# Hybrid decoder layer on one core: the MLP's first product as seven block products too, both products in one hand-ordered stream, weight sums formed by adding transfers

## The chip, the cores and the metric

One core of a Trainium2 chip runs the whole kernel. The metric is the device time of one execution in microseconds. The kernel before was run three times: median 786.67 us (785.09 to 787.71). Its profiled execution took 787.25 us, with a span of 785.5 us in the trace.

Engines: TensorE (PE; its weight loads are shown as PEld), VectorE (DVE), ScalarE (ACT), GpSimd (POOL), and SyncE (SP), which here only issues transfers. Sixteen transfer engines move data between the chip's memory and the on-chip SBUF.

## The reference, cut to what matters

The layer takes `x` (512 tokens x 1024), normalises it, multiplies by `w_in`, runs windowed attention and a convolution module side by side, merges both by gates, and adds `merged @ w_out` to `x`. Then comes the MLP, with a hidden width of 4096:

```python
x = x + merged @ w_out[l]
hmid = jnp.square(jax.nn.relu(rms_norm(x, norm_mlp_g[l]) @ w_ff1[l]))
x = x + hmid @ w_ff2[l]
```

All inputs are float32. The kernel works in float32r and splits each operand into a high part (a copy rounded by the cast) and a low part (the rest); a product is hi x hi + hi x lo + lo x hi, so three matmuls stand for one.

## The kernel before, in words

Up to the merge the kernel puts its steps on a list with `at(position, step)`; the list is sorted by position and every engine gets its instructions in that order. One unit of position is a quarter of a 24-matmul tile of TensorE. From `w_out` on, the code before is written stage after stage, and the framework's scheduler and its tile pools set the order on each engine.

*w_out.* 512 output columns at a time: four banks of PSUM collect 128 tokens each, 8 k-tiles x 3 matmuls with 512 moving columns. The second half goes token tile by token tile, each followed by `residual` (add to x, squares), `x2_norm` (the norm's factor in small steps on VectorE, then the scaling) and, for tiles 0 and 1, `x2_trans` (transposes on TensorE, then the high part on ScalarE and the low part on VectorE).

*MLP.* The hidden width is done in four parts of 1024 (`part`). Each part has a first-product stage and a second-product stage.

- First product (FF1): 8 tiles of 128 hidden channels, each the plain product over k = 8 tiles x 3 matmuls (`mm_T`, L187 to L192): weights are stationary, the 512 tokens move. The first three tiles (`EARLY`) are done in halves of 256 tokens, with the transposes of token tiles 2 and 3 between them. Weights arrive by `stationary_tiles` (L160), one 512 KB transfer per half of 256 columns, and are split by `split` (L153: cast on ScalarE, subtraction on VectorE). `ff1_evac` (L1125) takes relu, square, the parts and the sums `aS` of the activations that the next stage needs.
- Second product (FF2): a 2x2 block product of Winograd's form with seven multiplications instead of eight. Blocks: 256 tokens x 512 hidden x 512 outputs. `product` (L1175) issues one multiplication as 24 matmuls with 512 moving weight columns. Sums of weight blocks (`tq`, `b12`) are made on VectorE (`sub`, and L1214), then split by `pieces_of` (L1098). `add` (L1192) adds the banks to x, and in the last part stores the output.

Weights come in on SP's queue alone; GpSimd does nothing after w_out.

Of the kernel before, what the change touches and what calls it, by code (L numbers as in the profile page):

```python
# [52 lines left out]
def tile_hybrid_block(  # L53
# [941 lines left out]
    banks = ["ln", "ln", "ln", "mm", "mm", "mm"]  # L995

    def bank(name):

        banks.append(banks.pop(0))
        return pool_of["mm"].tile([P, S], F32, name=name, tag=banks[-1])  # L1000

    mTh, mTl = mT["h"], mT["l"]
    p2.close()
    gp.close()


    ff = ctx.enter_context(tc.tile_pool(name="ff", bufs=1, reuse_waits="tile"))

    def row4k(name, dtype=F32):
        return ff.tile([P, D], dtype, name=name, tag="row", bufs=5)  # L1010

    def quarter(name, dtype=F32):
        return ff.tile([P, 4, S], dtype, name=name, tag="quarter", bufs=4)

    gmlp = row4k("gmlp")
    nc.sync.dma_start(gmlp, bc(norm_mlp_g[0], P))
    x1 = []
    for t in range(NT):
        x1_t = keep.tile([P, D], F32, name=f"x1_{t}", tag="at", bufs=4)
        nc.sync.dma_start(x1_t, x[t * P:(t + 1) * P, :])  # L1020
        x1.append(x1_t)
    x2Th = ff.tile([P, KD, S], F32R, name="x2Th")
    x2Tl = ff.tile([P, KD, S], F32R, name="x2Tl")

    def mm_rows(accs, pieces, ah, al, kk):

        n = len(pieces)
        for i in range(n):
            for j in range(kk):
                for t in range(NT):  # L1030
                    k = i * kk + j
                    mm_M(accs[t], ah(k, t), al(k, t), pieces[i][0][:, j, :], pieces[i][1][:, j, :], k == 0,
                         k == n * kk - 1)

# [223 lines left out]
```

## Time and profile before

| | |
|---|---|
| three runs | 785.09 to 787.71 us, median 786.67 |
| profiled execution | 787.25 us, span 785.5 us |
| TensorE busy | 774.8 us, 99% of the span |
| VectorE, ScalarE, GpSimd busy | 561.5, 404.2, 254.3 us |
| moved by transfers | 79.56 MB, mean 101 GB/s |
| MLP: from its first to its last matmul | 451.86 to 781.43 us |

How to read it: a matmul's time in the trace runs from its start to its modelled end, and the next one starts before that end, so TensorE's busy time only says that work was always under way. The step from one start to the next tells its rate. "Idle before" is the time an engine stood still just before an instruction, with the work that ended last before it named behind the arrow.

### The profile page before, as it was taken

The numbers are of one execution on the slowest core, as the hardware profiler recorded it, in microseconds if no ns is written. First come the engines' busy times: TensorE is split into PE (matmuls) and PEld (weight loads), VectorE is DVE, ScalarE is ACT, GpSimd is POOL, SyncE is SP. The second block draws the span as 40 slices with busy tenths as digits, with TensorE's granted clock in tenths as the row PEclk, the third lists the DMA queues.
The fourth block names the chain that finished last, engine by engine and source line by source line (L and its number), as shares of the span: only waits on it lengthen the run. The fifth ranks groups of instructions, "written<-read, shape, count | busy, mean of one in ns | idle before, by whom it ended". The sixth has DMA issues, their size and how long they took to land.

```text
span 785.5 us, 10448 instructions
## 1 busy us (share of the span) xinstructions
PE 774.8 (99%) x3960; PEld 658.8 (84%) x3960; DVE 561.5 (71%) x949; ACT 404.2 (51%) x683; POOL 254.3 (32%) x189
## 2 busy tenths in 40 slices
PE   7999999999999999999999999999999999999998
PEld 7989989898888888888888898888888888888886
DVE  5466978898888878876431886886578766885683
ACT  5535557667666655356233356544554365435640
POOL 4443978958575565434364000000000000000000
PEclk8999999999999999999999999999999999999999
DMA  7351040314132131613335343143224223331102
GB/s 258 103 190 54 1 161 20 116 54 135 53 109 81 55 107 55 214 56 105 108 108 187 101 144 132 54 160 108 84 77 161 66 96 108 108 106 54 40 15 107
DMA packets 64807, 79.56 MB, mean 101 GB/s; under 512 B 2980, under 2 KB 52180, under 8 KB 64758
## 3 DMA queue, kind: packets, MB, share of 16 engines
q1 hardware_dynamic: 64758, 78.91, 29.9%
q8 instruction: 31, 0.51, 0.3%
q14 instruction: 18, 0.15, 0.1%
HBM read 76.78 MB, written 2.12 MB: 100 GB/s over the span
## 4 chain that ended last, share of the span: by engine, by line
PE 92%; DVE 3%; POOL 2%; ACT 1%; DMA 1%; issue 1%; SPq 0%; DVEq 0%; POOLq 0%; ACTq 0%
PE ps_f L191 7%; PE ps_f L192 7%; PE ps_f L190 7%; PE ps_x L1189 4%; PE ps_x L1186 4%; PE ps_x L1188 4%; PE ps_ta L484 2%; PE ps_ta L486 2%; PE ps_g L484 2%; PE ps_ta L485 2%; PE ps_wo L198 2%; PE ps_wo L196 2%; PE ps_wc L486 2%; PE ps_wc L484 2%; PE ps_y L1189 2%; PE ps_y L1186 2%
## 5 line engine op out<-in xcount | busy, mean ns | idle before, releaser
L782 DVE SCALAR_TENSOR_TENSOR cv<-h,wcol,cv 128x512 f32<-128x512 f32 x208 | 147.5, 746 | 0.5
L191 PE MATMUL ps_f<-x2Tl,wh_f 128*128 128x512 f32 (+1 forms) x280 | 104.1, 372 | 0.1
L190 PE MATMUL ps_f<-x2Th,wh_f 128*128 128x512 f32 (+1 forms) x280 | 103.6, 371 | 0.2 <-ACT x2Th L208 0.2
L192 PE MATMUL ps_f<-x2Th,wl_f 128*128 128x512 f32 (+1 forms) x280 | 103.8, 371 | 0.0
L157 DVE TENSOR_TENSOR wl_f<-raw_f,wh_f 128x1024 fp32r<-128x1024 f32 x32 | 39.1, 1223 | 59.8 <-ACT wh_f L156 58.8
L156 ACT CAST wh_f<-raw_f 128x1024 fp32r<-128x1024 f32 x32 | 33.6, 1054 | 55.4 <-PE ps_f L191 37.0
L191 PEld LDWEIGHTS ps_f<-x2Tl,wh_f 128*128 128x128 f32 x280 | 52.7, 188 | 9.3 <-DVE x2Tl L209 0.3
L190 PEld LDWEIGHTS ps_f<-x2Th,wh_f 128*128 128x128 f32 x280 | 52.6, 188 | 9.4 <-ACT x2Th L208 0.5
L192 PEld LDWEIGHTS ps_f<-x2Th,wl_f 128*128 128x128 f32 x280 | 52.7, 188 | 9.1
L1109 ACT CAST wh_b<-b 128x1024 fp32r<-128x1024 f32 x24 | 25.3, 1056 | 40.4 <-PE ps_y L1189 13.1
L1096 DVE TENSOR_TENSOR wl_b<-b,wh_b 128x1024 fp32r<-128x1024 f32 x24 | 29.3, 1223 | 22.1 <-ACT wh_b L1109 22.1
L1109 ACT CAST wh_t<-t 128x1024 fp32r<-128x1024 f32 x24 | 24.9, 1054 | 35.4 <-DVE t L1096 15.5
L691 ACT ACTIVATE s<-s,negm 128x257 f32<-128x257 f32 (+1 forms) x64 | 30.4, 478 | 16.5 <-DVE negm L683 16.5
L196 PE MATMUL ps_q<-wh_q,uTh 128*128 128x256 f32 x128 | 36.6, 286 | 0.0
L198 PE MATMUL ps_q<-wh_q,uTl 128*128 128x256 f32 x128 | 36.2, 283 | 0.0
L197 PE MATMUL ps_q<-wl_q,uTh 128*128 128x256 f32 x128 | 36.2, 283 | 0.0
L715 DVE TENSOR_TENSOR pTl<-ptp,pTh 128x512 fp32r<-128x512 f32 x28 | 19.3, 690 | 23.4 <-ACT pTh L711 23.4
L774 POOL TENSOR_TENSOR side<-side,tap 128x512 f32<-128x512 f32 x24 | 31.1, 1298 | 13.6 <-ACT tap L773 13.6
L1096 DVE TENSOR_TENSOR wl_t<-t,wh_t 128x1024 fp32r<-128x1024 f32 x24 | 29.0, 1220 | 5.9 <-ACT wh_t L1109 5.4
L700 POOL TENSOR_TENSOR s<-s,r 128x1024 f32<-128x1024 f32 (+1 forms) x16 | 26.9, 1682 | 14.7 <-DVE r L695 14.7
L683 DVE CUSTOM_DVE_ANT_0 s<-sp,bias,rb_sink 128x256 f32<-128x256 f32 (+1 forms) x64 | 26.2, 446 | 5.2 <-PE sp L676 4.9
L1096 DVE TENSOR_TENSOR aSl<-ss,aSh 128x1024 fp32r<-128x1024 f32 x16 | 19.6, 1225 | 13.2 <-ACT aSh L1122 13.2
(298 smaller groups left out, 2306.2 us busy)
## 6 DMA issues: line engine op xcount, KB each, us to landing
raw_f<-in_w_ff_dram SPq DMA_DIRECT2D x32, 512.0 KB, 4.2
b<-in_w_ff_dram SPq DMA_DIRECT2D x32, 512.0 KB, 3.8
x<-in_x_dram SPq DMA_DIRECT2D x8, 512.0 KB, 5.4
raw_g<-in_w_in_dram SPq DMA_DIRECT2D x8, 512.0 KB, 4.5
raw_a<-in_w_in_dram SPq DMA_DIRECT2D x8, 512.0 KB, 3.5
raw_q<-in_w_in_dram SPq DMA_DIRECT2D x8, 512.0 KB, 4.8
raw_ta<-in_w_in_dram SPq DMA_DIRECT2D x8, 512.0 KB, 4.4
raw_tc<-in_w_in_dram SPq DMA_DIRECT2D x8, 512.0 KB, 3.6
```

The lines of the kernel that those rows point to most:

```text
L157: lo_eng.tensor_tensor(out=wl, in0=raw_ap, in1=wh.bitcast(F32), op=ALU.subtract)
L190: pe.matmul(ps, wh[:, k, :], ah[:, k, cols], start=(k == 0), stop=False)
L191: pe.matmul(ps, wh[:, k, :], al[:, k, cols], start=False, stop=False)
L192: pe.matmul(ps, wl[:, k, :], ah[:, k, cols], start=False, stop=(k == nk - 1))
L196: pe.matmul(ps, ah, wh, start=first, stop=False)
L198: pe.matmul(ps, al, wh, start=False, stop=last)
L484: pe.matmul(ps, wh[:, k, :], ah(k), start=(k == 0), stop=False)
L782: ve.scalar_tensor_tensor(out=cps[ct], in0=src, scalar=w, in1=cps[ct], op0=ALU.mult, op1=ALU.add)
L1096: ve.tensor_tensor(out=out, in0=a, in1=b, op=ALU.subtract)
L1109: se.copy(wh, half)
L1186: pe.matmul(banks[t], ah, wh[:, j, :], start=(first and h + j == 0), stop=False, skip_group_check=True)
L1189: pe.matmul(banks[t], al, wh[:, j, :], start=False, stop=(last and h + j == 2), skip_group_check=True)
```

## The change

1. The first product of the MLP becomes a 2x2 block product with seven multiplications as well. A block is 512 k x 512 hidden x 256 tokens; weights stay stationary, so each matmul now moves 256 columns (before 512). The sums and differences of the activations (`xS`, from the transposed tokens `cx`) are made once; the results are collected in four blocks `ca`, on which relu, square, parts and sums are then taken.
2. Both products use one routine (`products`). The MLP is eight stages (`PHASES`): even ones first product, odd ones second. In each stage the seven products come in the order 1, 7, 6, 2, 5, 4, 3 (in the first stage 1, 2, 7, 6, 5, 4, 3).
3. Sums of weight blocks are no longer computed by VectorE. A block is fetched into one of three 1 MB buffers (`BUF`); when its two halves have been cut, a transfer from GpSimd's queue with `accum_op` adds another weight block onto the buffer, which gives the next product's weights. Products 5, 6, 4 and 7 get their weights that way; per stage there are 8 fetches and 8 adding transfers of 512 KB.
4. Everything from w_out on is put on the positions list. Pieces go through four slots (`n % 4`). The plain w_out chunks join the ring of weight chunks.
5. The norm before the MLP takes its factor from ScalarE's square root with one correction step (`rsqrt_root`), where before three steps on VectorE were made.

In the rows below, `aSh`, `aSl` are high and low part of the activations' sums, `xSh`, `xSl` those of the tokens, `piece` a cut weight half, `raw_b` and `raw_q` the three buffers, `c` a block of `ca`.

TensorE in the first part of the MLP, before: the end of one hidden tile and the start of the next (`wh_f`, `wl_f` weights, `x2Th`, `x2Tl` tokens).

```order
L190 MATMUL ps_f_6_4829<-x2Th,wh_f_3_0_4825 128x512
L191 MATMUL ps_f_6_4829<-x2Tl,wh_f_3_0_4825 128x512
L192 MATMUL ps_f_6_4829<-x2Th,wl_f_3_0_4826 128x512
L190 MATMUL ps_f_7_4863<-x2Th,wh_f_3_1_4859 128x512
L191 MATMUL ps_f_7_4863<-x2Tl,wh_f_3_1_4859 128x512
L192 MATMUL ps_f_7_4863<-x2Th,wl_f_3_1_4860 128x512
```

The same engine now, in a first-product stage: product 7, from its first bank to its second.

```order
L1133 MATMUL ps_y_4470<-xSh,pieceh 128x256
L1133 MATMUL ps_y_4470<-xSl,pieceh 128x256
L1133 MATMUL ps_y_4470<-xSh,piecel 128x256
L1133 MATMUL ps_y_4471<-xSh,pieceh 128x256
L1133 MATMUL ps_y_4471<-xSl,pieceh 128x256
L1133 MATMUL ps_y_4471<-xSh,piecel 128x256
```

The moving operand has half the columns, and one bank holds two hidden tiles of 256 tokens.

VectorE in the first second-product stage, before (`t` and `b` the buffers of weight sums, `wl_t`, `wl_b` low parts of weights, `ps_x`, `ps_y` the banks):

```order
L1196 TENSOR_TENSOR x_1_4106<-x_1_4106,ps_x_0_4909 128x512
L1096 TENSOR_TENSOR wl_t_01_5000<-t_4946,wh_t_01_4999 128x1024
L1096 TENSOR_TENSOR t_4946<-b_0_5018,t_4946 128x2048
L1196 TENSOR_TENSOR x_2_4108<-x_2_4108,ps_y_0_4910 128x512
L1196 TENSOR_TENSOR x_3_4110<-x_3_4110,ps_y_0_4911 128x512
L1096 TENSOR_TENSOR wl_t_00_5023<-t_4946,wh_t_00_5022 128x1024
L1096 TENSOR_TENSOR wl_t_01_5039<-t_4946,wh_t_01_5038 128x1024
```

VectorE now, at the passage from a first-product stage to a second-product stage:

```order
L1108 TENSOR_TENSOR piecel_4271<-raw_b,pieceh_4268 128x1024
L1155 TENSOR_TENSOR c_4155<-c_4155,ps_y_4470 128x512
L1155 TENSOR_TENSOR c_4155<-c_4155,ps_y_4471 128x512
L1108 TENSOR_TENSOR piecel_4272<-raw_b,pieceh_4269 128x1024
L1181 TENSOR_TENSOR c_4153<-c_4153,c_4155 128x1024
L1108 TENSOR_TENSOR piecel<-raw_q_4275,pieceh 128x1024
L1176 TENSOR_TENSOR aSl<-c_4153,aSh 128x4x256
L1186 SCALAR_TENSOR_TENSOR c_4153<-c_4153,c_4156 128x1024
L1108 TENSOR_TENSOR piecel_4270<-raw_q_4275,pieceh_4267 128x1024
```

The 2048-element weight sums are gone; between the cuts of the next stage's pieces stand the additions from PSUM and the sums and low parts of the activations.

The diff, cut to the MLP:

```diff
-    def sub(out, a, b):
-        ve.tensor_tensor(out=out, in0=a, in1=b, op=ALU.subtract)
...
-                mm_T(ps, wh, wl, x2Th, x2Tl)
-                ff1_evac(ps, m)
...
-        product(lambda t: a_of(aE, None, t), pieces_of(b11, f"b11_{part}"), X, True, True)
-        add(0, 0, X, False)
-        tq = quarter(f"t_{part}")
-        sub(tq, b22, b12)
-        product(S_(0), pieces_of(tq, f"t3_{part}"), Y, True, True)
-        add(1, 1, Y, False)
-        ve.tensor_tensor(out=tq, in0=tq, in1=b11, op=ALU.add)
...
+    ORDER = [(1, 2, 7, 6, 5, 4, 3)] + [(1, 7, 6, 2, 5, 4, 3)] * (PHASES - 1)
+    BUF = {1: 0, 5: 0, 7: 1, 6: 1, 4: 1, 2: 2, 3: 2}
...
+    def fetch(ph, buf, i, j, h):
+        ks = slice(2 * h, 2 * h + 2)
+        nc.sync.dma_start(tl["raw"][buf][:, ks, :], block(ph, i, j)[:, ks, :])
+
+    def fetch_add(ph, buf, i, j, h):
+        ks = slice(2 * h, 2 * h + 2)
+        ge.dma_start(tl["raw"][buf][:, ks, :], block(ph, i, j)[:, ks, :], accum_op=ALU.add)
...
+    def piece_hi(n, buf, h):
+        se.copy(tl["ph"][n % 4], tl["raw"][buf][:, 2 * h:2 * h + 2, :])
+
+    def piece_lo(n, buf, h):
+        ve.tensor_tensor(out=tl["pl"][n % 4], in0=tl["raw"][buf][:, 2 * h:2 * h + 2, :],
+                         in1=tl["ph"][n % 4].bitcast(F32), op=ALU.subtract)
...
+    def products(ph, prod, n, h, t):
+
+        (wh, wl), (ah, al) = (tl["ph"][n % 4], tl["pl"][n % 4]), operand(ph, prod)
+        acc = acc_of(ph, prod, t)
+        first = prod in (1, 7, 2) and h == 0
+        for c in range(2):
+            k = 2 * h + c
+            if ph % 2 == 0:
+                for q in range(2):
+                    o, w = acc[:, 256 * q:256 * q + 256], slice((2 * t + q) * P, (2 * t + q) * P + P)
+                    for i, (b, a) in enumerate(((wh, ah), (wh, al), (wl, ah))):
+                        pe.matmul(o, b[:, c, w], a[:, k, :], start=(first and c + q + i == 0),
+                                  stop=(k == 3 and i == 2), skip_group_check=True)
+            else:
+                w = slice(t * P, t * P + P)
+                for i, (a, b) in enumerate(((ah, wh), (ah, wl), (al, wh))):
+                    pe.matmul(acc, a[:, k, w], b[:, c, :], start=(first and c + i == 0),
+                              stop=(k == 3 and i == 2), skip_group_check=True)
...
+    for ph in range(PHASES):
+        m = M0 + 28 * ph
+        order = ORDER[ph]
+        ff1 = ph % 2 == 0
+        for j, prod in enumerate(order):
+            p = m + 4 * j
+            for h in range(2):
+                n = 2 * (7 * ph + j) + h
+                s = p - (3.4 if prod == 6 else 5.9) + 2 * h
...
+                at(s, piece_hi, n, BUF[prod], h)
+                at(s + 0.75, piece_lo, n, BUF[prod], h)
+                for t in range(2):
+                    at(p + 2 * h + t, products, ph, prod, n, h, t)
+                d = s + 0.9
+                more = ph + 1 < PHASES
+                if prod == 1:
+                    at(d, fetch_add, ph, 0, 0, 1, h)
+                elif prod == 7:
+                    at(d, fetch_add, ph, 1, 0, 0, h)
+                elif prod == 6:
+                    at(d, fetch_add, ph, 1, 1, 0, h)
+                elif prod == 2:
+                    at(d, fetch, ph, 2, 1, 1, h)
+                elif prod == 5 and more:
+                    at(d, fetch, ph + 1, 0, 0, 0, h)
+                elif prod == 4 and more:
+                    at(d, fetch, ph + 1, 1, 0, 1, h)
+                    at(d + 4.5, fetch_add, ph + 1, 1, 1, 1, h)
+                elif prod == 3 and more:
+                    at(d, fetch, ph + 1, 2, 1, 0, h)
...
-    nc = _bacc.Bacc("TRN2", target_bir_lowering=False, num_devices=1, dynamic_dma_scratch_size=1024)
+    nc = _bacc.Bacc("TRN2", target_bir_lowering=False, num_devices=1, dynamic_dma_scratch_size=2048)
```

In the loop above a product is four units long, `p` is its position, a piece is cut 5.9 units ahead (product 6: 3.4), and the transfer that refills the buffer is issued 0.9 units after that.

## Rows read from the trace of the kernel before

**Rows 1.** The page: span; busy us of each engine with its share of the span and its count of instructions; the chain that ended last, by engine.
```profile
span 785.5 us, 10448 instructions
...
PE 774.8 (99%) x3960; PEld 658.8 (84%) x3960; DVE 561.5 (71%) x949; ACT 404.2 (51%) x683; POOL 254.3 (32%) x189
...
PE 92%; DVE 3%; POOL 2%; ACT 1%; DMA 1%; issue 1%; SPq 0%; DVEq 0%; POOLq 0%; ACTq 0%
```

**Rows 2.** All that TensorE waited for from 400 us to the end: engine, tile and line, then the releaser, then us in total, times, longest.
```profile
PE ps_f L190 <- ACT x2Th L208: 0.2, 1, 0.2
```

**Rows 3.** Busy us (and instructions) of PE, PEld, DVE, ACT and POOL in stretches of the span; then TensorE's granted clock as a share of 2.4 GHz, the busy share of the transfer engines and what they moved in GB/s. The first rows are four of the eight stretches from 452 to 782 us (the others read alike) and the sum over all eight; the stretch from 498.55 is the first of the four second-product stages.
```profile
452.00:500.00 48.00, 47.89 (x287) 42.76 (x288) 36.12 (x56) 27.94 (x42) 0.00 (x0) 1.00 0.34 115
...
540.00:580.00 40.00, 40.00 (x178) 33.12 (x177) 22.48 (x31) 21.61 (x31) 0.00 (x0) 1.00 0.25 79
580.00:620.00 40.00, 40.00 (x178) 33.15 (x177) 34.49 (x36) 18.37 (x19) 0.00 (x0) 1.00 0.38 132
...
740.00:782.00 42.00, 41.59 (x184) 34.12 (x182) 28.85 (x34) 13.55 (x16) 0.00 (x0) 1.00 0.19 69
sum 330.00, PE 329.49 PEld 275.67 DVE 236.60 ACT 159.50 POOL 0.00; mean PE 41.19 PEld 34.46 DVE 29.58 ACT 19.94 POOL 0.00
...
498.55:536.64 38.09, 38.09 (x170) 31.55 (x169) 32.73 (x34) 17.29 (x18) 0.00 (x0) 1.00 0.39 135
```

**Rows 4.** Instructions of TensorE in order of time: start, us of one, engine, line, operation, tiles, shapes. First and last of 38 wide matmuls in a row of w_out; then first and last of 22 narrow ones in a row of the MLP's first product.
```profile
435.62 0.39 PE L197 MATMUL ps_wo<-wout1l,mTh 128*128 128x512 f32 x1
...
444.01 0.39 PE L198 MATMUL ps_wo<-wout1h,mTl 128*128 128x512 f32 x1
...
452.81 0.28 PE L192 MATMUL ps_f<-x2Th,wl_f 128*128 128x256 f32 x1
...
455.32 0.28 PE L192 MATMUL ps_f<-x2Th,wl_f 128*128 128x256 f32 x1
```

**Rows 5.** Groups of TensorE by line and shape over the whole span, count (x) | busy us, mean ns of one | idle before: the first product's matmuls, two of the three lines that are wide and two of the three that are narrow, and a weight load.
```profile
L190 PE MATMUL ps_f<-x2Th,wh_f 128*128 128x512 f32 x232 | 90.3, 389 | 0.0
L192 PE MATMUL ps_f<-x2Th,wl_f 128*128 128x512 f32 x232 | 90.2, 389 | 0.0
...
L191 PE MATMUL ps_f<-x2Tl,wh_f 128*128 128x256 f32 x48 | 13.8, 288 | 0.1
L190 PE MATMUL ps_f<-x2Th,wh_f 128*128 128x256 f32 x48 | 13.3, 285 | 0.2 <-ACT x2Th L208 0.2
...
L190 PEld LDWEIGHTS ps_f<-x2Th,wh_f 128*128 128x128 f32 x280 | 52.6, 188 | 9.4 <-ACT x2Th L208 0.5
```

**Rows 6.** TensorE in order of time around the first matmuls of the MLP (ps_f) and at the third group of transposes (tp_m, x8 together), columns as in rows 4.
```profile
450.59 1.03 PE L206 MATMUL tp_m<-ident,u 128*128 128x128 f32 x8
451.86 0.62 PE L190 MATMUL ps_f<-x2Th,wh_f 128*128 128x256 f32 x3 [0.24 <-ACT x2Th L208]
452.59 0.38 PE L191 MATMUL ps_f<-x2Tl,wh_f 128*128 128x256 f32 x1
...
455.44 1.04 PE L206 MATMUL tp_m<-ident,u 128*128 128x128 f32 x8
456.24 0.36 PE L191 MATMUL ps_f<-x2Tl,wh_f 128*128 128x256 f32 x1
```

**Rows 7.** The end of the span in order of time: the last matmul and the last addition.
```profile
781.20 0.39 PE L1189 MATMUL ps_x<-wh_b,aSl 128*128 128x512 f32 x1
781.63 0.69 DVE L1196 TENSOR_TENSOR x<-x,ps_x 128x512 f32<-128x512 f32 x1 [2.03 <-PE ps_x L1189]
```

**Rows 8.** Groups of VectorE by line and shape from 380 us on, columns as in rows 5.
```profile
L1096 DVE TENSOR_TENSOR wl_b<-b,wh_b 128x1024 fp32r<-128x1024 f32 x24 | 29.3, 1223 | 22.1 <-ACT wh_b L1109 22.1
...
L1196 DVE TENSOR_TENSOR x<-x,ps_x 128x512 f32<-128x512 f32 x32 | 21.2, 682 | 7.6 <-PE ps_x L1189 7.6
L1096 DVE TENSOR_TENSOR aSl<-ss,aSh 128x1024 fp32r<-128x1024 f32 x16 | 19.6, 1225 | 13.2 <-ACT aSh L1122 13.2
...
L1096 DVE TENSOR_TENSOR t<-b,t 128x2048 f32<-128x2048 f32 x4 | 9.2, 2292 | 0.1
...
L1069 DVE SCALAR_TENSOR_TENSOR u<-x,y_m,gmlp 128x1024 f32<-128x1024 f32 x4 | 5.1, 1285 | 0.1
...
L114 DVE TENSOR_TENSOR a_m<-y_m 128x1 f32<-128x1 f32 x12 | 1.9, 159 | 0.4
```

**Rows 9.** The same for ScalarE.
```profile
L156 ACT CAST wh_f<-raw_f 128x1024 fp32r<-128x1024 f32 x32 | 33.6, 1054 | 55.4 <-PE ps_f L191 37.0 <-PE ps_x L1189 10.0 <-PE ps_z L1189 5.0
...
L1131 ACT ACTIVATE r<-ps_f 128x512 f32<-128x512 f32 x32 | 19.2, 599 | 1.0
...
L1041 ACT ACTIVATE fsq<-x 128x512 f32<-128x512 f32 x8 | 5.0, 629 | 7.0 <-DVE x L1039 7.0
L208 ACT CAST x2Th<-tp_m 128x512 fp32r<-128x512 f32 x8 | 4.5, 585 | 12.4 <-PE tp_m L206 12.4
...
L1041 ACT ACTIVATION_READ_ACCUMULATOR fsq<-x 128x1 f32 x8 | 1.5, 186 | 0.0
```

**Rows 10.** Transfers by tile: count, KB each, median us from issue to landing.
```profile
raw_f<-in_w_ff_dram SPq DMA_DIRECT2D x32, 512.0 KB, 4.2
b<-in_w_ff_dram SPq DMA_DIRECT2D x32, 512.0 KB, 3.8
...
out_dram<-x SPq DMA_DIRECT2D x8, 256.0 KB, 2.0
```

More of the change, by code (lines that the diff above doesn't have):

```diff
@@ new lines, in tile_hybrid_block, with load_x1, bank, wout_mm @@
+    x1 = []
+    def load_x1():
+        for t in range(NT):
+            x1_t = keep.tile([P, D], F32, name=f"x1_{t}", tag="at", bufs=4)
+            nc.sync.dma_start(x1_t, x[t * P:(t + 1) * P, :])
+            x1.append(x1_t)
+    at(WO + 3, load_x1)
+    at(W0 + 0.9, open_tail)
+    banks = ["ln", "ln", "ln", "mm", "mm", "mm"]
+    def bank(name):
+        banks.append(banks.pop(0))
+        return pool_of["mm"].tile([P, S], F32, name=name, tag=banks[-1])
+    def wout_mm(acc, k, t, wh, wl):
+        cols = slice(t * P, (t + 1) * P)
+        mm_M(acc, mT["h"][:, k, cols], mT["l"][:, k, cols], wh, wl, k == 0, k == KD - 1)
@@ new lines, in x2_trans, with x2_keep @@
+    def x2_trans(t, half):
+        tp = aux.tile([P, 4, P], F32, name=f"tp_m{t}{half}", tag="aux")
+        for j in range(4):
+            k = 4 * half + j
+            pe.transpose(tp[:, j, :], us[t][:, k * P:(k + 1) * P], ident)
+        tl["tp", t, half] = tp
+    def x2_keep(t, half):
+        se.copy(tl["cx"][2 * (t // 2) + half][:, :, (t % 2) * P:(t % 2) * P + P], tl["tp", t, half])
+    for i, u in enumerate(wout_uses):
+        for j in range(2):
+            at(W0 + 4 * i + 2 * j, wout_first, u, i, j)
@@ new lines, in row_add, with c_half @@
+    def row_add(ph, half_t, half_n, prod, t, minus, store):
+        n, cols = 2 * half_t + t, slice(half_n * S, half_n * S + S)
+        ve.tensor_tensor(out=x1[n][:, cols], in0=x1[n][:, cols], in1=acc_of(ph, prod, t),
+                         op=ALU.subtract if minus else ALU.add)
+        if store and ph == PHASES - 1:
+            nc.sync.dma_start(out[n * P:(n + 1) * P, cols], x1[n][:, cols])
+    def c_half(i, t):
+        return tl["ca"][i].rearrange("p (t q) c -> p t (q c)", t=2)[:, t, :]
@@ new lines, in operands, with open_x @@
+    def operands(x, p):
+        for key, pos in p.items():
+            if key[0] == "S":
+                at(pos, op_sum, x, int(key[1]))
+            else:
+                at(pos, op_hi, x, int(key[1]))
+                at(pos + 0.75, op_lo, x, int(key[1]))
+    def open_x():
+        cx = keep.tile([P, 2, 4, 256], F32, name="cx2", tag="act", bufs=2)
+        tl["cx"] += [cx[:, i] for i in range(2)]
+        tl["xS"] = [tl["pool"].tile([P, 4, 4, 256], F32R, name=f"xS{n}", tag="xS" + n) for n in "hl"]
@@ new lines, in open_a, with open_banks @@
+    def open_a(what):
+        if what == "S":
+            tl["aS"] = [keep.tile([P, 4, 4, 256], F32R, name=f"aS{n}", tag="act", bufs=2) for n in "hl"]
+        else:
+            w = 256 if what == "E" else S
+            tl["a" + what] = [tl["pool"].tile([P, 4, w], F32R, name=f"a{what}{n}", tag=f"a{what}{n}") for n in "hl"]
+    def open_banks():
+        x, y, z = ([bank(f"ps_{role}{t}") for t in range(2)] for role in "xyz")
+        tl["banks"] = ({"x": x, "y": y, "z": z}, {"x": z, "y": y, "z": x})
@@ L994, in tile_hybrid_block @@
             fn(*args)
[L995 to L1033, printed above, removed]
```

323 lines of the change are left out of this document (171 added, 152 removed).

## The prediction

> **What bounds the kernel now.** I read the page's busy shares and chain first. TensorE is busy for 774.8 of 785.5 us, and the chain that ended last lies 92% on it [rows 1]. Next the list of what TensorE waited for, from 400 us on, where w_out and the MLP lie: one entry of 0.2 us [rows 2]. So in the part that the change rewrites there is no wait to remove; only fewer or cheaper matmuls help, and every new wait on TensorE costs its full length. The granted clock is 1.00, the 2.4 GHz level, from 452 us on [rows 3].
>
> Busy time is no measure of a matmul here, since its rows overlap (390 ns long, started every 227 ns). I take the step between starts. A matmul with 512 moving columns: from 435.62 to 444.01 us lie 37 steps, 8.39 / 37 = 0.2268 us. One with 256 columns: from 452.81 to 455.32 lie 21 steps, 2.51 / 21 = 0.1195 us, so two narrow ones cost 0.239 us, 5% more than a wide one [rows 4].
>
> The profiled execution took 787.25 us, 1.75 more than its span and 0.58 above the median of 786.67. I make the sum against 787.25 and take the 0.58 off at the end.
>
> **The change part by part.** *First product of the MLP.* Before: 696 wide and 144 narrow matmuls (x232 and x48 on each of three lines, [rows 5]): 696 x 0.2268 + 144 x 0.1195 = 157.9 + 17.2 = 175.1 us. After: 4 stages of 7 products of 2 halves x 2 banks x 2 k-tiles x 2 column blocks x 3 = 48 narrow matmuls, 1344 in all: 1344 x 0.1195 = 160.6 us. The columns fall by an eighth (12.5%), the time by 8.3%, because all of them are now narrow. **Gain 14.5 us.** The narrow step is read from the same operation on the same operands, so I take it with little doubt.
>
> *Second product.* 4 x 7 x 24 = 672 wide matmuls before and after: 152.4 us, unchanged. Transposes: 32 before and after.
>
> *Check of the sum.* From the first FF1 matmul at 451.86 [rows 6] to the step after the last matmul at 781.20 [rows 7] are 329.6 us; 175.1 + 152.4 + two groups of eight transposes at 0.8 (455.44 to 456.24, [rows 6]) are 329.1. Nothing else is in this stretch.
>
> *w_out and the norm,* now in the written order with the rest. 192 wide matmuls as before, none of them with a wait [rows 2], so nothing to gain. The one place where before lost time is the eight transposes at 450.59 and what follows: the second FF1 matmul starts only at 452.59 where 0.8 + 0.12 us would do, about 1 us lost [rows 6]. After, the first product needs only the first 256 tokens, which come from token tiles 0 and 1; for these I count from the end of tile 1's w_out matmuls: add 0.68, square 0.82, some eight small steps of 0.16, scaling 1.29, transposes, copy 0.59, hi 1.05, lo 1.22: about 8 us, while two more token tiles give TensorE 2 x 24 x 0.2268 = 10.9 us [rows 8, 9]. Tile 3's own chain of about 4.9 us to its transposes lies beside product 1 (5.7 us). So the start is covered with one to three microseconds to spare; I put the 1 us gained against small new waits here and book zero.
>
> *VectorE* [rows 8]. Per pair of stages before: 59 us by these lines (236.6 us busy in the 330 us of [rows 3], of which a pair is a quarter). After: 28 weight cuts x 1.22 = 34.2, 7 low parts and 4 sums of activations x 1.23 = 13.5, 6 + 14 additions from PSUM x 0.68 = 13.6: 61.3 us of a pair's 78.3. The four weight sums of 2.29 each leave VectorE, 14 more cuts come. In the second-product stage alone: 14 cuts 17.1, 14 additions 9.5, 8 operand steps 9.8 = 36.4 us in a stage of 38.1, against 32.7 before in 38.1 (498.55 to 536.64, [rows 3]). That is tight (96%), but a cut is placed to end about one product (5.4 us) ahead of its use and the following first-product stage asks only for about 25 of 40 us. Cost zero; if the cover fails, see the rivals. *ScalarE:* 28 casts x 1.05, 7 operand casts and 7 relu or square at 1.05, 8 PSUM reads of 0.6 = 49 of 78.3 us [rows 9]: hidden.
>
> *Transfers.* This is the new part. Before, a pair of stages loads 8 MB once; after, each stage fetches eight 512 KB halves and adds eight more, so 16 fetches and 16 adds per pair. A plain 512 KB transfer: in 580 to 620 us the engines moved 132 GB/s at a share of 0.38, so 347 GB/s when busy, 1.51 us of all 16 [rows 3]; it lands 3.8 us after issue [rows 10]. No adding transfer is in the trace. Bound from below: the same as a fetch, 1.51 and 3.8 us. From above: three passes one after the other (read the weights, read the tile, write it back), 4.5 and 11.4 us. I take two, since the nearest rows are a fetch and, for reading the tile, the output's store, 2.0 us for 256 KB [rows 10]: 3.0 us of the engines, and 3.8 + 2 x 2.0 = 7.8 us to landing.
> Throughput for a pair at two passes: 16 x 1.51 + 16 x 3.02 = 72.5 us against TensorE's 160.6 / 4 + 152.4 / 4 = 78.3. Hidden, with 7% to spare.
> The tightest link: product 7 and product 6 follow one another and use the same buffer. Product 7's piece can be cut once TensorE has left the slot, 1.5 products (8.2 us) before its use; less cast, cut and handoffs (1.05 + 1.22 + 0.2) its buffer is free for the add 5.7 us before product 7. Product 6 begins 5.4 us after that and needs its own 2.5 us of cutting: 5.7 + 5.4 - 2.5 = 8.6 us for the add, against 7.8. All other adds have one and a half times that or more. The adds are issued from GpSimd, which does nothing else then. Behind a late piece the cast waits on ScalarE and the cut on VectorE, and behind these the next product's pieces, so a late add shows in full on TensorE.
> The Trainium skill, "Collectives: The Full Stack", section on the bandwidth ceiling, has a rule against this: an add made in the transfer takes two source reads, and its reduce ran at 1/1.93 of a copy. An estimate by that figure: a pair would ask 24.2 x 2.93 = 70.9 us of 78.3, so the transfers would still be hidden, but with no room for a second transfer to be late. No run here shows it yet.
>
> *Tail.* Last matmul, one addition (0.69 at 781.63, [rows 7]), one 256 KB store: the same.
>
> *Sum:* 787.25 - 14.5 = 772.75; less 0.58 for the median 772.2; I add 0.8 for waits at eight stage changes of 0.1 each. **773.0 us.**
>
> **The rivals.**
> *A: the adds become the bound (slower).* Place: the 16 transfer engines in all eight stages. With r passes per add a pair asks 24.2 x (1 + r). It exceeds 78.3 from r = 2.24; the gain of 3.6 per pair is gone from r = 2.39. At 2.5: 84.7, 6.4 x 4 = 26 us, 773 + 26 = 799 us; at three: 96.8, 74 us, 847 us. For it: the traffic doubles in a stretch whose share is 0.19 to 0.38 so far, a quarter of the adds is on an 8.6 us link, and nothing in the trace shows their rate. Against it: at one or two passes everything fits.
> *B: VectorE's second-product stage falls behind.* If each of its 36 instructions waits 0.15 us more on handoffs, the stage needs 41.8 us; up to 3.7 us x 4 = 15 us. With half of it covered by the lead: 781 us. For it: 96% and an in-order queue in which additions from PSUM stand before cuts. Against it: before ran 32.7 of 38.1 without one wait on TensorE.
> *C: the narrow stream does not keep 0.1195 us.* At 0.1303 the gain is zero, 787 us. For it: the weight is exchanged at every narrow matmul, 188 ns of load beside a 120 ns step [rows 5]. Against it: 144 of just these ran at that step.
>
> **How the numbers follow.** Forecast 0.68 (its own range 769 to 777), B 0.18, A 0.12, C 0.02. Within 0.3% means 784.3 to 789.0, about what can be told from no change. Faster: 0.68 and 0.13 of B, 0.81. Same: 0.03 of B and C, 0.05. Slower: A and 0.02 of B, 0.14. The range from 769 to 792 leaves out A and a little below.
>
> **What would show it.** Right: narrow matmuls 0.1195 us apart throughout the first-product stages, 40.1 us per such stage and 38.1 per other; TensorE's waits under 3 us from w_out on; transfer share 0.6 to 0.95 in the MLP. A would show as ScalarE's casts waiting for the adding queue and TensorE waiting for casts, most at product 6. B would show as TensorE waiting for cuts late in second-product stages, with VectorE above 95% there. The forecast falls if a stage takes over 42 us, or if the adds land later than 8.6 us.

## The result and the profile after

The changed kernel takes 790.2 us, median of 19 runs (786.71 to 794.59), beside 786.68 us for the kernel before (19 runs): ratio 1.0042, 95% interval [1.0029, 1.0056]. It is slower by 3.5 us, where 773.0 us was forecast. Its profiled execution took 788.5 us.

The page of the changed kernel: span, busy time, two transfer queues (packets, MB, share of 16 engines' span), the chain that ended last, and transfers with KB and median us from issue to landing.

```profile
span 786.7 us, 11648 instructions
...
PE 766.4 (97%) x4464; PEld 668.5 (85%) x4464; DVE 566.0 (72%) x888; ACT 438.6 (56%) x696; POOL 332.1 (42%) x253
...
q1 hardware_dynamic: 56566, 78.91, 30.7%
q0 software_dynamic: 17408, 33.56, 24.2%
...
PE 59%; DMA 13%; issue 10%; DVE 8%; POOL 6%; ACT 3%; POOLq 0%; SPq 0%; ACTq 0%; DVEq 0%
...
raw_q<-in_w_ff_dram SPq DMA_DIRECT2D x48, 512.0 KB, 6.3
raw_q<-in_w_ff_dram POOLq DMA_DIRECT2D x48, 512.0 KB, 7.7
```

Against [rows 1]: TensorE's busy time fell by 8.4 us and its idle time rose by 9.6. The chain was 92% TensorE; now it is 59%, and transfers, VectorE and GpSimd are on it. GpSimd's queue (q0) carries the adds: 33.56 MB took 24.2% of 786.7 us, 190 us of all engines, 176 GB/s.

What TensorE waited for from 380 us on (us in total, times, longest):

```profile
PE ps_z L1138 <- DVE piecel L1108: 5.4, 6, 1.0
PE ps_x L1133 <- ACT c L1152: 2.2, 1, 2.2
PE ps_z L1138 <- ACT pieceh L1105: 1.7, 1, 1.7
PE ps_x L1133 <- DVE piecel L1108: 1.3, 3, 0.8
PE ps_x L1133 <- ACT pieceh L1105: 0.3, 1, 0.3
```

Before there was 0.2 us here [rows 2]; now 10.9 us. Nearly all but the 2.2 us stands at the two halves of product 6, which begin some 11 and 14 us after a stage's start (the 2.2 us stands before product 5 of the first stage). Who holds up the pieces, from the list of waits of the other engines in the MLP (same columns):

```profile
POOL raw_q L1094 <- DMA raw_q<-in_w_ff_dram: 139.9, 20, 13.3
...
DVE piecel L1108 <- ACT pieceh L1105: 69.7, 39, 6.6
ACT pieceh L1105 <- DMA raw_q<-in_w_ff_dram: 51.5, 20, 4.3
```

ScalarE's casts wait 51.5 us for blocks that are not there yet, VectorE's cuts wait for these casts, and TensorE for the cuts. Counted through in the program's order, all 20 of these waits are for products 7, 6 and 4, which share the second raw buffer.

The MLP's eight stages (columns as in [rows 3]: length, busy us of PE, PEld, DVE, ACT, POOL, clock, transfer share, GB/s), first and second product in turn:

```profile
453.65:496.80 43.15, 40.98 (x347) 40.78 (x346) 32.48 (x37) 28.44 (x36) 8.46 (x7) 1.00 0.63 134
496.80:539.62 42.82, 39.39 (x170) 31.42 (x169) 35.40 (x37) 24.21 (x26) 10.49 (x9) 1.00 0.90 203
539.62:581.02 41.40, 40.30 (x337) 39.88 (x336) 23.62 (x24) 24.43 (x28) 10.12 (x9) 1.00 0.92 211
581.02:621.01 39.99, 39.04 (x170) 31.42 (x169) 35.17 (x37) 22.00 (x24) 9.68 (x8) 1.00 0.91 205
621.01:661.34 40.33, 40.08 (x337) 39.87 (x336) 22.96 (x24) 24.52 (x27) 9.69 (x8) 1.00 0.92 211
661.34:702.29 40.95, 39.20 (x170) 31.42 (x169) 34.84 (x37) 22.04 (x23) 9.68 (x8) 1.00 0.90 204
702.29:742.65 40.36, 40.01 (x338) 39.60 (x336) 23.02 (x25) 24.51 (x28) 9.69 (x8) 1.00 0.93 213
742.65:782.70 40.05, 39.06 (x170) 31.23 (x168) 32.27 (x34) 18.87 (x20) 4.84 (x4) 1.00 0.64 146
sum 329.05, PE 318.06 PEld 285.62 DVE 239.76 ACT 189.01 POOL 72.66; mean PE 39.76 PEld 35.70 DVE 29.97 ACT 23.63 POOL 9.08
```

Forecast were 40.15 and 38.1 us, 313 in all; it is 329.05, as long as the 329.6 us before. The last second-product stage asks less of the transfers than the others (share 0.64) and still takes 40.05.

**The loop of one buffer.** The second raw buffer serves product 7, then (by an add) 6, then (by an add) 4; after that a fetch and another add make it product 7's block of the next stage. One turn of its second half, as ScalarE's casts of it show (in order of time; start, us, idle before and releaser):

```profile
623.02 1.05 ACT L1105 CAST pieceh<-raw_q 128x1024 fp32r<-128x1024 f32 x1 [3.02 <-DMA raw_q<-in_w_ff_dram]
...
633.57 1.05 ACT L1105 CAST pieceh<-raw_q 128x1024 fp32r<-128x1024 f32 x1 [0.91 <-DMA raw_q<-in_w_ff_dram]
...
644.64 1.05 ACT L1105 CAST pieceh<-raw_q 128x1024 fp32r<-128x1024 f32 x1 [2.06 <-DMA raw_q<-in_w_ff_dram]
...
663.63 1.05 ACT L1105 CAST pieceh<-raw_q 128x1024 fp32r<-128x1024 f32 x1
```

Product 7's cast waits 3.02 us for the add, product 6's 0.91, product 4's 2.06. The adds between them as GpSimd issues them (same columns; the last row is both halves of the next product 7's add), and the landing of the last two (least, median, most):

```profile
625.75 1.20 POOL L1094 DMA_DIRECT2D raw_q<-in_w_ff_dram  x1 [1.31 <-DVE piecel L1108]
...
636.29 1.21 POOL L1094 DMA_DIRECT2D raw_q<-in_w_ff_dram  x1 [1.69 <-DVE piecel L1108]
650.74 2.44 POOL L1094 DMA_DIRECT2D raw_q<-in_w_ff_dram  x2 [13.24 <-DMA raw_q<-in_w_ff_dram]
...
DMA to landing us min/median/max: 8.0/9.8/11.6
```

The second half's add, issued at 652.0, lands 11.6 us later at 663.6, and the next product 7's cast starts at 663.63. ScalarE shows no idle time there, since its other work ends at the same moment. The turn is 10.55 + 11.07 + 18.99 = 40.61 us, one link right behind the other, and the stage that it spans 40.33. Nothing in it may be late, since the next turn starts from its end.

From this came three theories. **Loop:** the turn of the second buffer sets the stage; transfers as such have room. **Full engines** (rival A of the prediction): at a share of 0.9 the adds cannot go faster. **Placement:** a smaller effect beside them. The unchanged convolution matmuls ahead of the MLP have a step of 0.2333 us in the trace after, 0.2267 before, and those of w_out 0.2300 against 0.2268. By the sizes of the tiles in the program, the large tiles of four pools start 192 bytes past a multiple of 256 in the changed kernel, where before all were at multiples; the traces hold no addresses, so this is tried by shifting the tiles.

### The profile page after: what moved, and what is told of

Read it like the earlier page. It is cut to its first block, busy times and chain, and to the rows that moved or that the text cites. A ratio compares the mean times of both kernels' runs of the same rounds, so it can differ in the third digit from the quotient of the medians.

```text
span 786.7 us, 11648 instructions
## 1 busy us (share of the span) xinstructions
PE 766.4 (97%) x4464; PEld 668.5 (85%) x4464; DVE 566.0 (72%) x888; ACT 438.6 (56%) x696; POOL 332.1 (42%) x253
## 3 DMA queue, kind: packets, MB, share of 16 engines
q0 software_dynamic: 17408, 33.56, 24.2%
## 4 chain that ended last, share of the span: by engine, by line
PE 59%; DMA 13%; issue 10%; DVE 8%; POOL 6%; ACT 3%; POOLq 0%; SPq 0%; ACTq 0%; DVEq 0%
DMA raw_q<-in_w_ff_dram 12%; DVE piecel L1108 4%; PE ps_x L1133 3%; POOL raw_b L1094 2%; POOL raw_q L1094 2%; PE ps_ta L492 2%; PE ps_wc L492 2%; PE ps_wc L493 2%; PE ps_wc L494 2%; PE ps_ta L494 2%; PE ps_wo L196 2%; PE ps_wo L198 2%; PE ps_ta L493 2%; PE ps_wo L197 2%; PE ps_g L492 2%
## 5 line engine op out<-in xcount | busy, mean ns | idle before, releaser
L1094 POOL DMA_DIRECT2D raw_q<-in_w_ff_dram x48 | 58.8, 1226 | 222.4 <-DMA raw_q<-in_w_ff_dram 139.9
L1108 DVE TENSOR_TENSOR piecel<-raw_q,pieceh 128x1024 fp32r<-128x1024 f32 x80 | 97.1, 1221 | 57.0 <-ACT pieceh L1105 56.9
L1105 ACT CAST pieceh<-raw_q 128x1024 fp32r<-128x1024 f32 x80 | 82.6, 1048 | 70.9 <-DMA raw_q<-in_w_ff_dram 51.5
L1108 DVE TENSOR_TENSOR piecel<-raw_b,pieceh 128x1024 fp32r<-128x1024 f32 x32 | 41.2, 1291 | 29.0 <-ACT pieceh L1105 29.0
L1133 PE MATMUL ps_x<-xSh,pieceh 128*128 128x256 f32 x192 | 54.3, 283 | 2.5 <-ACT c L1152 2.2
L1133 PE MATMUL ps_x<-xSh,piecel 128*128 128x256 f32 x192 | 54.5, 284 | 1.4 <-DVE piecel L1108 1.3
L1133 PE MATMUL ps_x<-xSl,pieceh 128*128 128x256 f32 x192 | 54.1, 282 | 0.0
L1138 PE MATMUL ps_z<-piecel,aSh 128*128 128x512 f32 x96 | 38.4, 400 | 5.4 <-DVE piecel L1108 5.4
L1105 ACT CAST pieceh<-raw_b 128x1024 fp32r<-128x1024 f32 x32 | 33.2, 1046 | 11.6 <-PE ps_y L1138 10.1
L1138 PE MATMUL ps_z<-pieceh,aSh 128*128 128x512 f32 x96 | 37.5, 391 | 1.7 <-ACT pieceh L1105 1.7
L1133 PEld LDWEIGHTS ps_x<-xSh,piecel 128*128 128x128 f32 x192 | 36.4, 190 | 2.2 <-DVE piecel L1108 2.2
L1138 PE MATMUL ps_z<-pieceh,aSl 128*128 128x512 f32 x96 | 37.5, 391 | 0.0
L1133 PEld LDWEIGHTS ps_x<-xSl,pieceh 128*128 128x128 f32 x192 | 36.4, 189 | 0.0
```

Of the source, the lines that this page charges most:

```text
L1094: ge.dma_start(tl["raw"][buf][:, ks, :], block(ph, i, j)[:, ks, :], accum_op=ALU.add)
L1105: se.copy(tl["ph"][n % 4], tl["raw"][buf][:, 2 * h:2 * h + 2, :])
L1108: ve.tensor_tensor(out=tl["pl"][n % 4], in0=tl["raw"][buf][:, 2 * h:2 * h + 2, :], in1=tl["ph"][n % 4].bitcast(F32), op=ALU.subtract)
L1133: pe.matmul(o, b[:, c, w], a[:, k, :], start=(first and c + q + i == 0), stop=(k == 3 and i == 2), skip_group_check=True)
L1138: pe.matmul(acc, a[:, k, w], b[:, c, :], start=(first and c + i == 0), stop=(k == 3 and i == 2), skip_group_check=True)
```

## The experiments

Each ran beside the kernel before on the same chip (medians of it 786.1 to 787.1 us). Ratios are to it. "The changed kernel, aligned" is the changed kernel with the edit of the first experiment.

**1 and 2: placement.** 64 bytes a partition more in a small tile should put the changed kernel's large tiles back on multiples of 256; 192 bytes more (`+ 48` in place of `+ 16`) should take those of the kernel before off.

```diff
-    sm.tile([P, LEAD // 4], F32, name="even", bufs=1)
+    sm.tile([P, LEAD // 4 + 16], F32, name="even", bufs=1)
```

> The changed kernel with 64 bytes more of padding in the small pool, so that all large tiles start on a multiple of 256 bytes again as in the kernel before (as changed, the tiles of the late pools start 192 bytes past one). Theory P (placement): the wide matmuls of the second gated tile stage (ps_wc) go back from 0.2333 to 0.2268 us a step, which is 192 x 0.0065 = 1.3 us; those of the attention output by about 0.8 us; the wide MLP stages from 0.2298 to 0.2268, 672 x 0.003 = 2 us; a cut from raw_b from 1.29 to 1.22 us. In all 3 to 5 us less than the changed kernel: 785 to 787 us. Theory L (late adds): the waits at product 6 stay, some 8 to 11 us of waits on TensorE. Rival: steps are set by something else than the start address, then nothing moves and the time stays at 790.

> The kernel before with 192 bytes more of padding in the same pool, so that its late tiles start 192 bytes past a multiple of 256. Theory P: ps_wc goes from 0.2268 to about 0.233 us a step, the first product of the MLP (x2Th, x2Tl move from such tiles) from 0.2268 to 0.23 or more, together 192 x 0.0065 + 696 x 0.0035 to 0.0065 = 4 to 6 us: 790 to 793 us. If placement is not the cause: 786.7 us.

Measured: 787.78 us, ratio 1.0012 [0.9999, 1.0024], for the changed kernel aligned; 796.43 us, 1.0123 [1.0107, 1.0140], for the kernel before shifted. The first and the last of 100 convolution matmuls in a row in the shifted kernel, then of 95 in the kernel before, from TensorE's rows in order of time:

```profile
384.80 0.39 PE L486 MATMUL ps_wc<-sTh,wl_wc 128*128 128x512 f32 x1
...
407.89 0.40 PE L486 MATMUL ps_wc<-sTh,wl_wc 128*128 128x512 f32 x1
...
384.62 0.39 PE L485 MATMUL ps_wc<-sTl,wh_wc 128*128 128x512 f32 x1
...
405.93 0.39 PE L486 MATMUL ps_wc<-sTh,wl_wc 128*128 128x512 f32 x1
```

23.09 / 99 = 0.2332 us a step, against 21.31 / 94 = 0.2267 before, without any wait and at a granted clock of 1.00. So the start of a tile costs up to 3% of a 512-column matmul, and 9.7 us of the kernel before. In the changed kernel it costs 2.4 us (790.2 to 787.8). There its second-product stages grow only from 38.1 to 38.5 us by it, and its 256-column matmuls do not suffer (0.1184 us shifted, 0.1200 aligned; both from the traces of experiments 5 and 6). TensorE's waits stay, 9.5 us in total. Placement is real and is the smaller part.

**3: no add between products 7 and 6.** This kernel leaves one weight block out of the sums of products 6 and 4.

```diff
                 elif prod == 7:
-                    at(d, fetch_add, ph, 1, 0, 0, h)
+                    pass
```

> The changed kernel without the two adding transfers per stage between product 7 and product 6 (that weight block is left out of the sums of products 6 and 4). Theory L: the waits at product 6 vanish; TensorE's waits in the MLP fall from 10.9 us to under 3 and the time to 778 to 781 us. Theory S (all 16 transfer engines are saturated, whichever add it is): only 2 of 16 transfers go, the share stays near 0.85 and the time falls by under 3 us, to 787 or more.

Measured: 777.55 us, ratio 0.9887 [0.9865, 0.9910], 12.65 below the changed kernel. The waits at product 6 are down to one of 1.0 us; from the third stage on stages take 39.78 and 38.51 us. The remaining adds still land after 7.4 and 8.1 us. One add fewer of four a stage was enough, though this takes away load as well as a link, so it does not yet part the two theories.

**4: the same transfers, copying instead of adding.** This kernel leaves out all sums of weight blocks.

```diff
-        ge.dma_start(tl["raw"][buf][:, ks, :], block(ph, i, j)[:, ks, :], accum_op=ALU.add)
+        ge.dma_start(tl["raw"][buf][:, ks, :], block(ph, i, j)[:, ks, :])
```

> The changed kernel with the same transfers from GpSimd's queue, but copying instead of adding (all sums of weight blocks are left out). If the addition itself is dear (its 33.6 MB took 24.2% of the 16 engines' span, 176 GB/s, against 327 GB/s for the fetches): the share falls from 0.9 to about 0.7, these transfers land after some 5 us instead of 7.7, the waits at product 6 vanish, time 778 to 781. If the issue from GpSimd or the doubled traffic is what is late: share and landing stay, 788 to 790 us.

Measured: 775.36 us, ratio 0.9854 [0.9839, 0.9869]. Its page, columns as above:

```profile
q0 software_dynamic: 9216, 33.56, 13.4%
...
raw_q<-in_w_ff_dram POOLq DMA_DIRECT2D x48, 512.0 KB, 4.4
raw_b<-in_w_ff_dram POOLq DMA_DIRECT2D x16, 512.0 KB, 5.1
```

The same bytes take 13.4% of 772.8 us, 103.6 us, instead of 190.4: an add costs 1.84 copies, and lands after 7.7 us instead of 4.4. TensorE waits 0.9 us in all. So the adding is what the change pays for, 14.8 us with placement unchanged, and the seven-product stream itself runs as forecast: the gain is there in the matmuls.

**5 and 6: a fourth raw buffer.** Products 7, 6 and 4 alternate between two buffers from stage to stage, and the next stage's block is fetched and added to earlier. All adds stay.

```diff
+        raw_c = pool.tile([P, 4, S], F32, name="raw_c")
...
+    def buf_of(ph, prod):
+        return 3 if BUF[prod] == 1 and ph % 2 else BUF[prod]
...
-                    at(d, fetch, ph + 1, 1, 0, 1, h)
-                    at(d + 4.5, fetch_add, ph + 1, 1, 1, 1, h)
+                    at(m + 9 + 2 * h, fetch, ph + 1, buf_of(ph + 1, 7), 0, 1, h)
+                    at(m + 15.5 + 2 * h, fetch_add, ph + 1, buf_of(ph + 1, 7), 1, 1, h)
```

> The changed kernel with a fourth raw buffer of 1 MB: products 7, 6 and 4 use the second buffer in even stages and the new one in odd stages, and the next stage's block for product 7 is fetched and added to during the stage before it rather than in its last part. No transfer is taken away or made shorter. Loop theory (the second buffer passes cast, add, cast, add, cast, fetch, add once a stage and sets the stage): stages fall to about 38.5 and 40 us as in the kernel that copied, some waits of 1 to 2 us stay at product 6 behind its add, and the time is about 776 to 780 us. Rival, the DMA engines are simply full (share 0.9): stages stay at 40 to 41 us whatever the buffers do, time 785 to 790 us.

> The same fourth buffer, with 64 bytes of padding a partition so that the large tiles start at multiples of 256 bytes again. Loop theory and placement theory together: 2 to 3 us below the kernel without the padding, of which most lies ahead of the MLP and in the steps of 512 columns (0.2268 instead of 0.2333 us). If placement is worth nothing once the waits are gone, the two are equal within 1 us.

Measured: 777.79 us, ratio 0.9888 [0.9873, 0.9903]; aligned 775.61 us, 0.9863 [0.9849, 0.9878]. Loop and placement each held their number: 12.4 and 2.2 us. Steady stages are 39.78 and 38.51 us shifted, 40.31 and 38.1 aligned, 78.3 and 78.4 a pair: inside the MLP placement is worth nothing net, and in these two traces the aligned one gains its time ahead of it (MLP start at 450.45 against 454.29 us).

**7 and 8: one sum a stage made by an engine.** Product 6's sum is taken from two raw buffers on VectorE (7) or, with `ge` for `ve`, on GpSimd (8); three buffers, aligned.

```diff
+    def raw_sum(h):
+        ks = slice(2 * h, 2 * h + 2)
+        ve.tensor_tensor(out=tl["raw"][1][:, ks, :], in0=tl["raw"][1][:, ks, :], in1=tl["raw"][0][:, ks, :],
+                         op=ALU.add)
...
-                if prod == 1:
-                    at(d, fetch_add, ph, 0, 0, 1, h)
-                elif prod == 7:
-                    at(d, fetch_add, ph, 1, 0, 0, h)
+                if prod == 7:
+                    at(d, raw_sum, h)
+                    at(d + 0.3, fetch_add, ph, 0, 0, 1, h)
```

> The changed kernel, aligned, in which the sum for product 6 is made by VectorE from two raw buffers (two instructions of 128x1024 a stage) instead of by an adding transfer; the adding transfer for product 1 follows it on the same buffer. Loop theory: one of the three adds leaves the loop of the second buffer (7.7 us becomes about 2.5 us), so the stage falls to about 38.5 to 40 us and the time to 776 to 781 us. Rival, VectorE is full in the second product's stage (36.4 us of work in 38.1, now about 41): that stage goes to 41 us, and the time stays at 785 to 792 us.

> The same sum for product 6 made by GpSimd. Loop theory: as with VectorE, 776 to 781 us, if GpSimd does a 128x1024 sum in about 2.5 us. Rival, GpSimd's sum is several times slower than VectorE's, or delays the adding transfers that GpSimd issues behind it: the wait at product 6 stays or grows, 787 us or more.

Measured: VectorE 781.42 us, ratio 0.9934 [0.9910, 0.9958], just above what the loop theory gave; its later stages take 40.31 and 38.7 us, so VectorE has the room. Its first stage took 45.7 us. TensorE stands still there for 2.2 us before product 5, and right behind that its granted clock is 0.50, the 1.2 GHz level, for over 3 us (columns as in [rows 3]):

```profile
476.50:479.10 2.60, 0.63 (x6) 0.43 (x4) 1.81 (x3) 1.45 (x3) 0.00 (x0) 0.99 1.02 281
479.20:482.40 3.20, 3.11 (x14) 3.11 (x15) 1.94 (x2) 0.54 (x3) 0.00 (x0) 0.50 1.08 285
```

In that stretch a narrow matmul takes a step of 0.214 us (480.10 to 481.81, eight steps). In the trace of the changed kernel a wait of 2.2 us at the same place was not followed by such a fall; what decides it is open.

GpSimd 789.60 us, 1.0047 [1.0031, 1.0064]: the rival of its expectation. Groups of that kernel (count, busy us, mean ns, idle before), GpSimd's sum and two of VectorE's:

```profile
L1098 POOL TENSOR_TENSOR raw_q<-raw_q,raw_b 128x1024 f32<-128x1024 f32 x16 | 47.9, 2996 | 94.2 <-DVE piecel L1113 94.1
...
L1113 DVE TENSOR_TENSOR piecel<-raw_q,pieceh 128x1024 fp32r<-128x1024 f32 x70 | 91.3, 1313 | 31.6 <-ACT pieceh L1110 31.6
...
L1191 DVE SCALAR_TENSOR_TENSOR c<-c,c 128x1024 f32<-128x1024 f32 x8 | 18.1, 2266 | 0.1
```

A sum takes GpSimd 3.0 us (2.4 to 3.4), and VectorE's own instructions stretch beside it: 2266 ns in the mean where experiment 7 has 1222, the cuts 1313 against 1221. The means mix two cases: four of the eight instructions of L1191 ran beside a sum and took 3.31 us each, the other four 1.22; of the cuts seven ran beside one.

**9: crowding instead of the loop?** The fourth buffer of 5 and 6 also spread the transfers out. Here, with three buffers and aligned, product 1's two adds go behind product 7's, so that the add for product 6 has no other just ahead of it.

```diff
                 if prod == 1:
-                    at(d, fetch_add, ph, 0, 0, 1, h)
+                    at(m + 1.2 + 0.3 * h if ph else d, fetch_add, ph, 0, 0, 1, h)
```

> The changed kernel with three raw buffers, aligned, in which the two adding transfers that turn product 1's block into product 5's are issued behind the two that turn product 7's into product 6's, instead of ahead of them (from the second stage on). The loop of the second buffer is left as it is. Crowding theory (the add for product 6 is late because product 1's adds go through the engines just ahead of it): product 6's add lands in 6 to 6.5 us, the waits at product 6 go, and the time falls to 777 to 781 us. Loop theory (three adds and a fetch on one buffer take a stage's length): the add for product 6 gets faster, but the next stage's block for product 7 still comes late, so stages stay within 1 us of 41.5 and 40 us and the time at 783 to 788 us.

Measured: 790.59 us, ratio 1.0038 [1.0018, 1.0057]. Not faster than the aligned kernel, and 2.6 us slower than the loop theory had it. TensorE waits 13.2 us. In the fourth stage, the two adds for product 6 and then the two for product 4 (nanoseconds that an issue takes, first and last start; landing, least, median and most):

```profile
L1094 POOL DMA_DIRECT2D raw_q<-in_w_ff_dram x2: 1206/1214/1222, 584.3 to 587.9; - x2
DMA to landing us min/median/max: 5.7/5.7/5.8
...
L1094 POOL DMA_DIRECT2D raw_q<-in_w_ff_dram x2: 1203/1208/1212, 594.0 to 597.0; - x2
DMA to landing us min/median/max: 10.0/10.7/11.3
```

The adds for product 6 did land sooner: after 5.4 to 7.7 us from the second stage on, against 6.3 to 8.5 in the aligned kernel. But those for product 4, which now have product 1's adds just ahead of them, land after 9.1 to 12.3 us instead of 6.7 to 9.4. So crowding is real, but it only moved from one link of the turn to the next. Stages still take 40.0 to 42.9 us: a faster add for product 6 alone is worth nothing, and crowding at that place is out as the cause.

**10: the fourth buffer alone.** As 6, with fetch and add at the places of the changed kernel.

```diff
-                    at(m + 9 + 2 * h, fetch, ph + 1, buf_of(ph + 1, 7), 0, 1, h)
-                    at(m + 15.5 + 2 * h, fetch_add, ph + 1, buf_of(ph + 1, 7), 1, 1, h)
+                    at(d, fetch, ph + 1, buf_of(ph + 1, 7), 0, 1, h)
+                    at(d + 4.5, fetch_add, ph + 1, buf_of(ph + 1, 7), 1, 1, h)
```

> The fourth buffer, aligned, but with the next stage's fetch and add at the places in the program where the changed kernel has them; only the wait for product 4's cut is gone from that fetch. Loop theory: the buffer alone is what counts, the fetch goes out as soon as SP reaches it, and the time is 776 to 779 us. If the earlier place counts (the adds spread over the stage rather than crowded at its end), 780 to 786 us.

Measured: 776.0 us, ratio 0.9866 [0.9834, 0.9899], the same as 6. All that TensorE waited for from 380 us on:

```profile
PE ps_x L1139 <- ACT c L1158: 1.6, 1, 1.6
PE ps_z L1144 <- DVE piecel L1114: 1.2, 2, 1.0
```

Its stages, from the second to the sixth:

```profile
496.07:535.96 39.89, 38.72 (x171) 31.39 (x170) 36.47 (x38) 23.63 (x25) 10.94 (x9) 1.00 0.98 221
535.96:576.27 40.31, 40.31 (x338) 40.31 (x336) 23.10 (x24) 25.07 (x28) 9.71 (x8) 1.00 0.91 210
576.27:614.38 38.11, 38.11 (x171) 31.54 (x170) 34.92 (x37) 21.78 (x23) 9.75 (x8) 1.00 0.97 221
614.38:654.69 40.31, 40.31 (x338) 40.31 (x337) 23.09 (x24) 25.12 (x28) 9.72 (x8) 1.00 0.90 209
654.69:692.79 38.10, 38.10 (x170) 31.54 (x169) 34.89 (x37) 21.76 (x23) 9.75 (x8) 1.00 0.98 222
```

From the third stage on TensorE is busy for the whole of each, and the engines carry more than in the changed kernel (share 0.90 to 0.98, there 0.90 to 0.93) without one wait. The next product 7's adds now take even longer, 11.4 to 14.6 us from the second stage to the seventh, and no cast waits for them. That settles it between the theories: no add was removed, shortened or moved in the program, only the tie to the buffer's last reader was cut, and 11.8 us went (787.78 to 776.0). Full engines are out as the cause.

**11: both.** Fourth buffer as in 6, and product 1's adds behind product 7's as in 9.

> Fourth buffer with the earlier fetch and add, aligned, and product 1's adds behind product 7's. If crowding still costs waits at product 6 in the first second-product stage (2.1 us above the others there), they shrink and the time is 773 to 775 us; if not, it stays at 775 to 776 us; if product 5's block is now late, TensorE waits at product 5 and the time is over 777 us.

Measured: 777.83 us, ratio 0.9883 [0.9856, 0.9909]: not better than 6. The first second-product stage is down to 38.13 us, as hoped, but the first stage takes 44.75 instead of 43.16. As in experiment 7 the granted clock falls to 0.50 behind the wait before product 5, here of 1.8 us:

```profile
479.10:482.30 3.20, 3.20 (x17) 3.20 (x17) 1.45 (x2) 0.51 (x2) 0.00 (x0) 0.50 1.10 216
```

At 0.214 us a step instead of 0.120 some 15 matmuls lose about 1.4 us in it (an estimate), most of the difference. Over the span the granted clock was 0.993 to 0.997 in the four runs of 11 and 0.998 to 1.000 in those of 6, so what the later adds alone are worth stays open.

The kernels of experiments 6 and 10, with all their sums by adding transfers, are the fastest that leave no work out: 775.61 and 776.0 us, 1.4% below the kernel before.

## Why the prediction was wrong

The forecast was 773.0 us and faster; it became 790.2 and slower, inside the range (769 to 792) but on the side that got 0.14. The 17.2 us between them are 11.8 for the loop (experiments 1 and 10), 2.4 for placement (the changed kernel and 1), and 3.0 that stay in experiment 10.

- *Gain in the first product, 14.5 us:* right. The narrow step is 40.31 / 336 = 0.1200 us (aligned) with 0.1195 forecast. Undisturbed stages take 40.31 and 38.1 us with 40.15 and 38.1 forecast.
- *Price of an add:* right. Two passes were taken; 1.84 were measured. The estimate by the Trainium skill, "Collectives: The Full Stack", section on the bandwidth ceiling, has an add at 1.93 copies, and the trace agrees within 5%.
- *Landing of an add,* put at 7.8 us: right in the median (7.7), partly by luck. It was added up from rows at a share of 0.38 and measured at 0.9, where a fetch takes 6.3 us instead of 3.8. It also holds for the adds for 6 and 4 only (6.0 to 9.0 from the second stage on); product 1's adds take 8.8 in the median and the next product 7's up to 11.8. So two signs that the prediction had named against itself came: adds later than 8.6 us, and stages of over 42 us (the first two).
- *"Hidden, with 7% to spare":* right. With the fourth buffer the share is 0.90 to 0.98 in the full stages, and TensorE does not wait.
- *The tightest link, "8.6 us for the add against 7.8":* right as far as it goes. In experiment 10 the adds on the two buffers land after 7.0 and 7.9 us in the median and product 6 waits 1.2 us in the whole MLP. But the 8.6 hold only if product 7's piece is cut on time.
- **"All other adds have one and a half times that or more": this step failed.** Each add was measured against its own gap, from the place where the program wants its block to be free. The adds for 6, for 4 and for the next 7 follow each other on one buffer, with a fetch between, and the gaps of a chain that closes on itself cannot be added up freely. By the prediction's own numbers a turn is three adds of 7.8, three times cast, cut and handoffs of 2.47, and a fetch of 3.8: 34.6 of a stage's 38.1 to 40.15 us. That is a tenth to spare, not half. In the turn shown above the three adds took 7.8, 8.3 and 11.7 us to the next cast, 27.8 instead of 23.4, the fetch (issued at 647.0) 5.0 instead of 3.8, and cast, cut and handoffs 7.8 in all: 40.6 us. The landing under the load of the change itself was not asked for. In the second-product stages product 4's cast moreover starts 1.2 to 1.8 us behind its block's landing, in ScalarE's order. Whatever is late in one turn is late in the next.
- *w_out "zero":* wrong for another reason than weighed. The steps of its 192 matmuls grew by the tiles' start, which the diff does not name, 0.6 us of the 2.4; of the rest, part lies in the convolution and the attention's output, which the sum has as unchanged. The trace of the changed kernel has no new wait there; those of experiments 3 and 5 have one of 2.2 and one of 0.5 us at the transposes ahead of the MLP. The wait of 2.2 us at the first stage's products 6 and 5 was not foreseen either: in that stage's order they stand next to each other and share their banks, so 5 must wait until ScalarE has copied 6.
- *Rival A* named the symptom word for word (casts waiting for the adding queue, TensorE at product 6) but gave it a cause, too little throughput, that is not there. It began at 2.24 passes; by its own sum it does not come at the measured 1.84. A chance for "late, though not full" was missing, and the 0.14 was too low for that.
- *Rival B:* did not come. VectorE needs 34.9 us of a 38.1 us second-product stage (36.4 forecast) with no wait on TensorE, and experiment 7 put 2.4 us more on it. *Rival C:* the step of 0.1303 us did not come.

The 3.0 us that stay in experiment 10 are not parted by a run. In its trace the first two stages are 4.6 us longer than the later ones (43.13 + 39.89 against 40.31 + 38.11). Of this 0.8 are eight transposes on TensorE, which the sum has; 1.6 is the wait before product 5 in the first stage, 1.2 the waits at product 6 in the second, and for waits the forecast had 0.8. The kernel that copied still waits 0.9 us before product 5, so more than half of that wait is not the adds' doing. Ahead of the MLP the granted clock was 0.50 from 340.5 to 343.7 us, where it is 1.00 in the trace of experiment 6, whose MLP starts 2.5 us sooner. How the rest divides was not tried.

## What to carry to other kernels

Where a buffer is refilled in place several times a round (read, add, read, add, read, fetch, add), add up the whole turn, with landings under the load that the change itself makes, and hold it against the round: single links that each have room can close into a loop that has none. Here one more buffer then gave 12.4 us, nearly as much as making every add a copy (14.8), and one faster link gave nothing. A share of 0.9 on the transfer engines did not say who waits (the kernel of experiment 10 has as much, with hardly a wait); TensorE's list of waits and the casts' releasers did. Compare the steps of code that was not changed, too: here they moved, and the placement of tiles had moved.
